# When the copies and the accumulations of summed weights are issued in a decoder layer, and how many splits stand ahead of the last pass's early sums

## The chip, the cores and the metric

The kernel runs on one core of a Trainium2 chip. Its time is in microseconds (us) of device time. TensorE does the matrix products, ScalarE and VectorE (ACT and DVE in the profile) the elementwise work, GpSimd (POOL) some of it and the DMAs that add while they write. SyncE (SP) issues nearly all other DMAs. All DMAs of the core run on the same 16 DMA engines.

## What is computed

One layer of a decoder, 256 tokens wide 2048, all in float32:

```python
h = rmsnorm(x, pre_mix_g);  proj = h @ w_in          # 2048 -> 4368 columns
o_a = sliding-window attention, o_b = forgetting attention, each rms-normalised
x = x + rmsnorm(concat(o_a, o_b) @ w_out, post_mix_g)
h = rmsnorm(x, pre_ffn_g)
u = causal_dwconv(h @ w_up, conv_w, conv_b)          # 2048 -> 2 * 5632
gate, val = split(u)
y = (gelu(gate) * val) @ w_down                      # 5632 -> 2048
out = x + rmsnorm(y, post_ffn_g)
```

## The kernel before

**Split weights.** TensorE works on pairs of reduced floats: each weight tile is loaded raw (float32, `w_load`, L88), ScalarE casts it to a high part (L143 in `w_split`, L343 in `split`), VectorE subtracts to get the low part (L146, L344), and a product is high by high, high by low and low by high. Five raw buffers and five pairs of split buffers turn in rings, so loads run ahead of TensorE until a ring is full. TensorE's order is the program's (`manual_schedule`, L48); the other engines are ordered by the framework's scheduler, apart from stretches that fix the order by hand: ScalarE, VectorE and GpSimd from L826 up to the first gate, and ScalarE, VectorE and SyncE from the last w_up group through the two column passes (L1199).

**The stages.** w_in: a start stage of four steps, then `proj_T` (L274) and plain loops (L662) for the three kinds of projection, with the attention of earlier heads woven in by `tick` and `later`. w_out: `out_half` (L735) twice; its last columns are done in a hand-ordered stretch (L826 to L873) in which `evac_b` (L763) scales and squares, GpSimd multiplies by the gain (L769), `mix_rstd` (L780) makes the reciprocal root (L214 on GpSimd), `residual` (L785) adds x (L787 on VectorE) and `turn` (L789) transposes on TensorE (L794). Then, twice, for one half of the 5632 rows each: eleven groups of w_up (`proj_T4`, L303: 32 high products at L315 and 32 low ones at L321 with four loads of 512 KB), each with a convolution (ScalarE L935, VectorE L937, GpSimd L938, ScalarE L942, VectorE L948 and L950), and after them two passes over w_down, one for each half of its columns (`column_pass`, L1017). While x goes into its next use, `x_dram` is written from ScalarE's queue (L991).

**Pair sums.** In a column pass rows come in pairs of 128-row blocks, eleven pairs to a half. For the six pairs in `FAST` seven block products are done in place of eight (`seven`, L1057), which needs sums of weight blocks. These are made in DRAM by DMA: `make_sums` (L70) returns eight steps for one pair. With b11, b12 (first block, left and right columns) and b21, b22 (second block), four copies on SyncE (L80) put b11, b22, b22 and b21 into t1, t3, t2 and t4, and four accumulating DMAs on GpSimd (L83) add b12 to t1, b12 to t3, t1 to t2 and t2 to t4. A full step moves 512 KB; in the first half t2 and t4 take only the first column pass, 256 KB.

**When a step is begun.** `w_load` counts its loads. From the 13th on, five loads of thirteen are followed by one step of the list `sum_steps`, copies and accumulations mixed in the order in which they depend on each other:

```python
        loads[0] += 1
        if loads[0] > SKIP and loads[0] * 5 % 13 < 5 and sum_steps and not paused[0]:
            tc.keep_in_program_order(sum_steps.pop(0)())
```

`paused` is set in the column passes, so no step is begun there, though their loads are counted. Loads 1 to 73 belong to w_in, 74 to 105 to w_out, 106 to 109 to the first gate; a half of w_up has 80 or more.

**The last pass.** Each pair is made ready by `prepare` (L1033): load, cast, subtract. In the second half's second pass the pairs go in the order 0, 2, 4, 1, 5, 6, 7, 3, 8, 9, 10, and the last three (`HOLD`) are kept: their products are done at the end, one output block after the other (`block`, L1094), so that blocks finish one by one. After the last fast pair (7), `ahead` makes the next two pairs ready, then `early_sums` (L1150) folds four banks into the output: a copy on ScalarE (L1161) and eight additions on VectorE (L1162 to L1169). The remaining pairs are made ready when the loop reaches them. Then VectorE adds bank 3 (L1240) and `down` (L1226) adds a block (L1229) and squares it on ScalarE (L1230); GpSimd multiplies by the last gain (`gain`, L1250, at L1253), `rstd_y` (L1264) makes `ry` (L1268), and `finish` (L1271) writes out.

Of the kernel before, what the change touches and what calls it, by code (L numbers as in the profile page):

```python
# [12 lines left out]
ALU = mybir.AluOpType  # L13
# [11 lines left out]
NEG = -1e30  # L25
FHALF = 22
HOLD = 3
SKIP = 12
FAST = (0, 2, 4, 5, 6, 7)


# [1 line left out]
def hybrid_layer(ctx: ExitStack, tc: tile.TileContext, x, pre_mix_g, w_in, b_forget, sinks,  # L33
# [3 lines left out]
    pe, act, dve, pool, sp = nc.tensor, nc.scalar, nc.vector, nc.gpsimd, nc.sync  # L37
# [12 lines left out]
    def bank(tag="acc"):  # L50
        return ps.tile([P, 512], F32, tag=tag, bufs=4, name="bank_" + tag)
# [13 lines left out]
    UNIT = 1024  # L65
    WB = 5

    pair_sums, sum_steps, loads, paused = {}, [], [0], [False]

    def make_sums(half, u):  # L70
        k = half * FHALF + 2 * u
        chunks = slice(0, 2) if half else slice(0, 1)
        t13, t24 = (tc.dram_tile([P, D], F32, name=n) for n in ("t13", "t24"))
        pair_sums[half, u] = t13, t24
        (t1, t3), (t2, t4), (b11, b12), (b21, b22) = (
            [w.rearrange("p (s x c) -> p s x c", s=2, x=2)[:, :, x, :] for x in range(2)]
            for w in (t13, t24, *(w_down[(k + a) * P:(k + a + 1) * P, :] for a in range(2))))

        def put(to, src, ch=slice(0, 2)):
            return lambda: sp.dma_start(to[:, ch, :], src[:, ch, :])  # L80

        def add(to, src, ch=slice(0, 2)):
            return lambda: pool.dma_start(to[:, ch, :], src[:, ch, :], accum_op=ALU.add)  # L83

        return [put(t1, b11), put(t3, b22), add(t1, b12), add(t3, b12), put(t2, b22, chunks),
                put(t4, b21, chunks), add(t2, t1, chunks), add(t4, t2, chunks)]

    def w_load(src, a, c, pin=False):  # L88
        raw = wp.tile([P, UNIT], F32, tag="raw", bufs=5, name="raw")
        i = sp.dma_start(raw[:, :a * c].rearrange("p (a c) -> p a c", a=a), src)  # L90
        if pin:
            tc.keep_in_program_order(i)
        loads[0] += 1
        if loads[0] > SKIP and loads[0] * 5 % 13 < 5 and sum_steps and not paused[0]:
            tc.keep_in_program_order(sum_steps.pop(0)())
        return raw, a, c

    last = []
    for half in range(2):
        for u in FAST:  # L100
            steps = make_sums(half, u)
            sum_steps += steps[:2] + last + steps[2:7]
            last = steps[7:]
    sum_steps += last

    LOW = 56

# [43 lines left out]
    def w_unit(src, a, c, keep=None):  # L151
        return w_split(w_load(src, a, c), keep=keep)
# [193 lines left out]
    with tc.tile_pool(name="mixp", bufs=1) as mp:  # L346
# [407 lines left out]
        hold = tc.tile_pool(name="hold", bufs=1)  # L754
# [61 lines left out]
        def out_cols(n, t, cs):  # L816
            b = bank()
            for k, hi, lo in kept[n]:
# [7 lines left out]
        order = tc.manual_schedule(engines={mybir.EngineType.Activation, mybir.EngineType.DVE,  # L826
                                            mybir.EngineType.Pool})
# [50 lines left out]
    with tc.tile_pool(name="ffn", bufs=1) as fp:  # L878
# [132 lines left out]
        def product(b, lh, ll, rhs, cols, first, last, to=None):  # L1011
            hi, lo = rhs
            for i, (a, r) in enumerate(((lh, hi), (lh, lo), (ll, hi))):
                pe.matmul(b[:, to] if to else b, a, r[:, cols], start=(first and i == 0),  # L1014
                          stop=(last and i == 2))

        def column_pass(G, sums, weights, some, order, k00, c0, load, parts, hold=1):  # L1017
# [7 lines left out]
            def of(k, t):  # L1025
                return G[k][:, t * P:(t + 1) * P], G[k][:, 256 + t * P:256 + (t + 1) * P]

            def first(bk):
                new = id(bk) not in started
                started.add(id(bk))  # L1030
                return new

            def prepare(u):  # L1033
                k = k00 + 2 * u
                if u not in some:
                    return [parts(load(w_rows(w_down, k + a, 1, c0, UNIT)), UNIT)
                            for a in range(2)]
                b11 = parts(load(w_rows(w_down, k, 1, c0, 512)), 512)
                w13, w24 = (w[:, c0:c0 + UNIT].rearrange("p (a c) -> p a c", a=1)
                            for w in weights[u])  # L1040
                r13 = load(w13)
                r2 = load(w_rows(w_down, k + 1, 1, c0, UNIT))
                f13 = parts(r13, UNIT)
                if ready_sums:
                    r24 = load(w24)
                else:
                    r24 = r13
                    dve.tensor_tensor(r24[:, left], r2[:, right], r13[:, left], op=ALU.add)
                    dve.tensor_tensor(r24[:, right], r2[:, left], r24[:, left], op=ALU.add)
                b2 = parts(r2, UNIT)  # L1050
                return b11, f13, b2, parts(r24, UNIT)

            def ahead(*us):
                for u in us:
                    ready[u] = prepare(u)
# [18 lines left out]
            def run(add_early):  # L1074
                early, late = ([bank(tag) for _ in range(4)] for tag in ("acc", "att"))
                banks.extend(zip(late, (0, 0, 1, 1), (left, right, left, right)))
                for i, u in enumerate(order):
                    forms = ready.pop(u) if u in ready else prepare(u)
                    if u in some:
                        seven(u, forms, *early, *late[:3])  # L1080
                        if u == fast[-1]:
                            ahead(*order[i + 1:i + 3])
                            add_early(*early)
                    elif i >= len(order) - hold:
                        held.extend((2 * u + a, forms[a]) for a in range(2))
                    else:
                        for a in range(2):
                            for bk, t, cols in banks:
                                product(bk, *of(2 * u + a, t), forms[a], cols, first(bk),
                                        hold > 1 and bk is late[3] and a == 1 and  # L1090
                                        u == plain[-1])
                return late
# [54 lines left out]
        def y_of(t, n):  # L1147
            return y_sb[:, t, n * 512:(n + 1) * 512]
# [24 lines left out]
        for half in range(2):  # L1173
# [5 lines left out]
            for g in range(FHALF // 2):  # L1179
# [36 lines left out]
                if g in FAST:  # L1216
                    i = FAST.index(g)
# [15 lines left out]
            for n, (_, run, block) in zip((0, 2), passes):  # L1233
# [8 lines left out]
                for i in range(4):  # L1242
# [4 lines left out]
                    else:  # L1247
                        dve.tensor_tensor(y_of(t, n + c), late[i], y_of(t, n + c), op=ALU.add)

        def gain(t, n, h=None, into=None):  # L1250
            cs = slice(0, 512) if h is None else slice(h * 256, h * 256 + 256)
            ys = y_sb[:, t, n * 512:(n + 1) * 512][:, cs]
            pool.tensor_tensor(ys if into is None else into, ys,  # L1253
                               gbf[n][:, cs], op=ALU.mult)
# [50 lines left out]
        last = fp.tile([P, 256], F32, tag="last", name="last")  # L1305
# [42 lines left out]
```

## Time and profile before

| what | us |
|---|---|
| median of 3 runs | 1058.95 (1058.43 to 1059.29) |
| the profiled execution | 1059.58 |
| its span, first to last instruction | 1057.9 |
| TensorE busy | 1043.1 |
| VectorE busy | 836.6 |
| ScalarE busy | 651.9 |
| GpSimd busy | 265.7 |

DMA engines moved 266.87 MB, 252 GB/s on average. TensorE's granted clock was 0.997 of full speed over the span.

The profile is one execution. A row of the timeline has start, duration, engine, line, operation, what is written from what, how many of them were merged, and in brackets how long the engine had been idle before and what ended that. A row of the waits has who waited for whom, the us in total, how often, and the longest. The chain of waits is followed back from the last instruction: at each step to what released it, or to the instruction before it on its engine. Queue q1 carries SyncE's DMAs, q0 those of GpSimd (the accumulations), q10 ScalarE's.

### The profile page before, as it was taken

To read this page: it belongs to the slowest core of one execution; us is meant where nothing else is said; L and a number is where in the kernel's file an instruction comes from. 1 tells how busy PE (TensorE), PEld (TensorE's weight loads), DVE (VectorE), ACT (ScalarE), POOL (GpSimd) and SP (SyncE) were. 2 spreads that over 40 slices of the span, in tenths; PEclk is the share of its full clock that TensorE was granted. 3 is DMA by queue.
4 is the path that set the end of the run, shared out by engine and by line. 5 is a ranking of instruction groups with operands and counts; after the bars stand their busy time and mean duration, and the time that the engine had idled before them with its cause. 6 is when DMAs were issued, how large, how long until landed. Compare 5 with 4: busy or idle time off the path is not lost.

```text
span 1057.9 us, 16559 instructions
## 1 busy us (share of the span) xinstructions
PE 1043.1 (99%) x5866; PEld 907.9 (86%) x5866; DVE 836.6 (79%) x1353; ACT 651.9 (62%) x1116; POOL 265.7 (25%) x304
## 2 busy tenths in 40 slices
PE   9999999999999999999999999999999999999995
PEld 7899988888888988888888888888888888888884
DVE  5989887887377797788796799857878788779885
ACT  6767667676466665665565666546555565558661
POOL 3254435442114132232231000013232231210005
PEclk9999999999999999999999999999999999999998
DMA  8768987977887999898989786879899897669792
GB/s 289 249 161 238 232 251 216 228 223 202 272 288 178 300 246 291 237 291 231 263 262 275 274 344 228 269 223 261 264 252 299 240 250 214 198 203 409 253 399 87
DMA packets 183806, 266.87 MB, mean 252 GB/s; under 512 B 9100, under 2 KB 133292, under 8 KB 182828
## 3 DMA queue, kind: packets, MB, share of 16 engines
q1 hardware_dynamic: 171200, 241.12, 69.0%
q0 software_dynamic: 11520, 22.02, 13.3%
q10 hardware_dynamic: 1004, 2.68, 0.7%
q8 instruction: 46, 0.75, 0.3%
q14 instruction: 36, 0.29, 0.1%
HBM read 261.45 MB, written 48.25 MB: 293 GB/s over the span
## 4 chain that ended last, share of the span: by engine, by line
PE 84%; DMA 5%; DVE 5%; issue 2%; ACT 2%; POOL 1%; SPq 0%; DVEq 0%; POOLq 0%; ACTq 0%
PE bank_acc L315 16%; PE bank_att L315 14%; PE bank_att L1014 11%; PE bank_acc L321 8%; PE bank_att L321 7%; PE bank_acc L284 7%; PE bank_acc L340 7%; PE bank_acc L1014 5%; PE bank_acc L289 4%; DMA raw<-in_w_out_dram 3%; PE bank_att L506 1%; DVE wlo L146 1%; PE bank_att L541 1%; DMA raw<-t 1%; PE bank_acc L977 1%
## 5 line engine op out<-in xcount | busy, mean ns | idle before, releaser
L146 DVE TENSOR_TENSOR wlo<-raw,whi 128x1024 fp32r<-128x1024 f32 (+3 forms) x271 | 336.6, 1254 | 109.0 <-ACT whi L143 101.1
L143 ACT CAST whi<-raw 128x1024 fp32r<-128x1024 f32 (+3 forms) x270 | 273.7, 1029 | 122.0 <-issue 42.7
L938 POOL TENSOR_TENSOR room<-room,rowf 128x256 f32<-128x256 f32 x88 | 96.5, 1116 | 357.6 <-DVE room L937 356.2
L315 PE MATMUL bank_acc<-hT,whi 128*128 128x512 f32 x736 | 173.3, 390 | 0.0
L315 PEld LDWEIGHTS bank_acc<-hT,whi 128*128 128x128 f32 x736 | 136.4, 188 | 27.4
L315 PE MATMUL bank_att<-hT,whi 128*128 128x512 f32 x640 | 150.6, 390 | 0.0
L315 PEld LDWEIGHTS bank_att<-hT,whi 128*128 128x128 f32 x640 | 118.7, 188 | 23.9
L1014 PE MATMUL bank_att<-whi,G 128*128 128x512 f32 x298 | 98.1, 389 | 0.0
L942 ACT ACTIVATE room<-room,cw 128x256 f32<-128x256 f32 x88 | 52.6, 601 | 67.5 <-POOL room L938 67.4
L321 PEld LDWEIGHTS bank_acc<-hT,wlo 128*128 128x128 f32 x736 | 89.3, 188 | 2.0
L321 PE MATMUL bank_acc<-hT,wlo 128*128 128x256 f32 x736 | 89.9, 279 | 0.0
L284 PE MATMUL bank_acc<-hT,whi 128*128 128x512 f32 x352 | 88.0, 395 | 0.0
L340 PE MATMUL bank_acc<-whi,oT 128*128 128x512 f32 (+1 forms) x272 | 81.8, 379 | 0.0
L321 PEld LDWEIGHTS bank_att<-hT,wlo 128*128 128x128 f32 x640 | 77.6, 188 | 1.7
L321 PE MATMUL bank_att<-hT,wlo 128*128 128x256 f32 x640 | 77.9, 279 | 0.0
L948 DVE SCALAR_TENSOR_TENSOR room<-room,cw 128x256 f32<-128x256 f32 x88 | 60.2, 687 | 18.3 <-ACT room L942 18.3
L344 DVE TENSOR_TENSOR wlo<-raw,whi 128x1024 fp32r<-128x1024 f32 (+1 forms) x61 | 66.7, 1117 | 8.8 <-ACT whi L343 7.8
L284 PEld LDWEIGHTS bank_acc<-hT,whi 128*128 128x128 f32 x352 | 63.3, 188 | 11.5
L343 ACT CAST whi<-raw 128x1024 fp32r<-128x1024 f32 (+1 forms) x61 | 57.5, 966 | 19.0 <-DMA raw<-in_w_down_dram 7.0
L1014 PEld LDWEIGHTS bank_att<-whi,G 128*128 128x128 f32 x298 | 55.9, 188 | 11.6
L340 PEld LDWEIGHTS bank_acc<-whi,oT 128*128 128x128 f32 x272 | 50.2, 188 | 9.4
L1014 PE MATMUL bank_att<-wlo,G 128*128 128x512 f32 x149 | 58.0, 389 | 0.0
(269 smaller groups left out, 1722.6 us busy)
## 6 DMA issues: line engine op xcount, KB each, us to landing
raw<-in_w_up_dram SPq DMA_DIRECT2D x176, 512.0 KB, 5.3
raw<-in_w_in_dram SPq DMA_DIRECT2D x51, 512.0 KB, 5.5
raw<-in_w_down_dram SPq DMA_DIRECT2D x49, 512.0 KB, 6.3
t<-in_w_down_dram SPq DMA_DIRECT2D x36, 512.0 KB, 6.9
raw<-in_w_out_dram SPq DMA_DIRECT2D x32, 512.0 KB, 6.9
t<-in_w_down_dram POOLq DMA_DIRECT2D x24, 512.0 KB, 10.8
raw<-t SPq DMA_DIRECT2D x18, 512.0 KB, 4.7
spare<-t SPq DMA_DIRECT2D x13, 512.0 KB
```

The lines of the kernel that those rows point to most:

```text
L143: i1 = act.copy(hi[:, cs], raw[:, cs])
L146: i2 = dve.tensor_tensor(lo[:, cs], raw[:, cs], hi[:, cs].bitcast(F32), op=ALU.subtract)
L284: pe.matmul(b, parts[u][0][:, a, m * P:(m + 1) * P], hT[:, kt, :], start=(kt == 0), stop=(kt == KT - 1))
L315: pe.matmul(b, parts[u][0][:, a, m * P:(m + 1) * P], hT[:, kt, :], start=(kt == 0), stop=(kt == KT - 1))
L321: pe.matmul(b[:, 256:512], parts[u][1][:, a, m * P:(m + 1) * P], hT[:, kt, 0:256], start=False, stop=False)
L340: pe.matmul(b, a, r[:, cols], start=(first and i == 0), stop=(last and i == 2))
L343: act.copy(hi, src)
L344: dve.tensor_tensor(lo, src, hi.bitcast(F32), op=ALU.subtract)
L938: pool.tensor_tensor(u[:, 2:258], u[:, 2:258], rowf, op=ALU.mult)
L942: act.activation(y, u[:, 2:258], AF.Identity, bias=cw[:, 3, ch:ch + 1], scale=cw[:, 2, ch:ch + 1])
L948: dve.scalar_tensor_tensor(y, u[:, 1:257], cw[:, 1, ch:ch + 1], y, op0=ALU.mult, op1=ALU.add)
L1014: pe.matmul(b[:, to] if to else b, a, r[:, cols], start=(first and i == 0), stop=(last and i == 2))
```

## The change

Copies and accumulations get a list each. A list is served only while the count of loads lies in a span, and each load there pays in a pace (9/8 or 9/16), counted in 256 KB; a step is begun when what is owed reaches its size (2, or 1 for the half steps). The copies' span is loads 13 to 90, the accumulations' loads 112 to 281, and these need the copies to be all begun. Loads of the column passes are no longer counted. Within the accumulations the last one of a pair (t2 to t4) stands behind the first one of the next pair.

In the pass with `hold` above 1, the second half's second, `ahead` now makes the next four pairs (3, 8, 9 and 10) ready ahead of the early sums, in place of two.

```diff
-SKIP = 12
+COPIES = (13, 91, 9 / 8)
+ADDS = (112, 282, 9 / 16)
...
         def put(to, src, ch=slice(0, 2)):
-            return lambda: sp.dma_start(to[:, ch, :], src[:, ch, :])
+            return ch.stop, lambda: sp.dma_start(to[:, ch, :], src[:, ch, :])
...
-        return [put(t1, b11), put(t3, b22), add(t1, b12), add(t3, b12), put(t2, b22, chunks),
-                put(t4, b21, chunks), add(t2, t1, chunks), add(t4, t2, chunks)]
+        copies.extend([put(t1, b11), put(t3, b22), put(t2, b22, chunks), put(t4, b21, chunks)])
+        return [add(t1, b12), add(t3, b12), add(t2, t1, chunks), add(t4, t2, chunks)]
+
+    def begin_some(steps, span):
+        begin, end, pace = span
+        if begin <= loads[0] < end:
+            owed[span] = owed.get(span, 0) + pace
+            while steps and owed[span] >= steps[0][0]:
+                size, step = steps.pop(0)
+                owed[span] -= size
+                tc.keep_in_program_order(step())
...
-        loads[0] += 1
-        if loads[0] > SKIP and loads[0] * 5 % 13 < 5 and sum_steps and not paused[0]:
-            tc.keep_in_program_order(sum_steps.pop(0)())
+        loads[0] += not paused[0]
+        if not paused[0]:
+            begin_some(copies, COPIES)
+            if not copies:
+                begin_some(adds, ADDS)
...
-            sum_steps += steps[:2] + last + steps[2:7]
-            last = steps[7:]
-    sum_steps += last
+            adds += steps[:1] + last + steps[1:3]
+            last = steps[3:]
+    adds += last
...
                         if u == fast[-1]:
-                            ahead(*order[i + 1:i + 3])
+                            ahead(*order[i + 1:i + (5 if hold > 1 else 3)])
                             add_early(*early)
```

More of the change, by code (lines that the diff above doesn't have):

```diff
@@ L66, in hybrid_layer @@
     WB = 5
-    pair_sums, sum_steps, loads, paused = {}, [], [0], [False]
+    pair_sums, loads, paused = {}, [0], [False]
+    copies, adds, owed = [], [], {}
     def make_sums(half, u):
@@ L79, in put @@
         def put(to, src, ch=slice(0, 2)):
-            return lambda: sp.dma_start(to[:, ch, :], src[:, ch, :])
+            return ch.stop, lambda: sp.dma_start(to[:, ch, :], src[:, ch, :])
         def add(to, src, ch=slice(0, 2)):
-            return lambda: pool.dma_start(to[:, ch, :], src[:, ch, :], accum_op=ALU.add)
-        return [put(t1, b11), put(t3, b22), add(t1, b12), add(t3, b12), put(t2, b22, chunks),
-                put(t4, b21, chunks), add(t2, t1, chunks), add(t4, t2, chunks)]
+            return ch.stop, lambda: pool.dma_start(to[:, ch, :], src[:, ch, :],
+                                                   accum_op=ALU.add)
+        copies.extend([put(t1, b11), put(t3, b22), put(t2, b22, chunks), put(t4, b21, chunks)])
[8 more added lines that the diff above has]
+                tc.keep_in_program_order(step())
     def w_load(src, a, c, pin=False):
@@ L1248, in hybrid_layer @@
                         dve.tensor_tensor(y_of(t, n + c), late[i], y_of(t, n + c), op=ALU.add)
+        assert not copies and not adds
         def gain(t, n, h=None, into=None):
```

## The prediction

> **What bounds the kernel now.** I read the page's first part, then TensorE's own waits, then the chain of waits around each of them, then the single engines in order of time.
>
> ```profile
> span 1057.9 us, 16559 instructions
> ## 1 busy us (share of the span) xinstructions
> PE 1043.1 (99%) x5866; PEld 907.9 (86%) x5866; DVE 836.6 (79%) x1353; ACT 651.9 (62%) x1116; POOL 265.7 (25%) x304
> ```
>
> A busy 99% proves little by itself, since the ends of matmuls are modelled. This is the whole list of what TensorE waited for (us in total, times, longest):
>
> ```profile
> PE bank_acc L200 <- DVE junk L195: 1.3, 1, 1.3
> PE bank_att L1014 <- DVE more L344: 1.2, 1, 1.2
> PE bank_acc L365 <- DMA x_in<-in_x_dram: 0.9, 1, 0.9
> PE bank_att L794 <- DVE x_sb L787: 0.6, 1, 0.6
> PE bank_att L553 <- DVE pl L344: 0.5, 1, 0.5
> PE bank_att L365 <- DMA x_in<-in_x_dram: 0.4, 1, 0.4
> ```
>
> Six waits, 4.9 us. Three (L200, L365 twice, 2.6 us) belong to the start, before any weight sum begins. L794 comes just before w_up, L1014 in the last pass; L553 is a busy stretch of VectorE in the projections. The change removes no matmul, so it can win only what lies in L794, L553 and L1014, and can lose wherever it makes TensorE wait anew. No w_up or w_down product waited, though DMA has much to do there. The profiled execution took 1059.58 us, 1.68 us over its span; the median of the runs is 1058.95. I work out differences on the profiled one and subtract them from the median.
>
> **Part 1: what leaves the stretch before w_up.** Until now every load up to the end of w_up could be followed by a copy or an accumulation. Afterwards the copies go with loads 13 to 90 and the accumulations with loads from 112. Loads 1 to 73 are w_in, 74 to 105 w_out, 106 to 109 the first gate units. So GpSimd issues no DMA in the projections and w_out at all. It did, on the chain that ends in the wait at L794:
>
> ```profile
> 319.04 2.61 POOL t L83 x3
> 321.65 2.57 POOL mix_sb L769 x2
> 324.22 0.53 POOL rmix L214
> 324.75 0.02 issue
> 324.77 0.76 DVE x_sb L787
> ...
> 329.77 0.87 PE bank_att L794 x8
> ```
> ```profile
> 324.56 0.39 PE L340 MATMUL bank_acc<-whi,oT 128*128 128x512 f32 x1
> 325.58 0.99 PE L794 MATMUL bank_att<-ident,x_sb 128*128 128x128 f32 x5 [0.63 <-DVE x_sb L787]
> ```
> ```profile
> 320.94 0.63 ACT L768 ACTIVATE junk<-mix_sb 128x512 bf16<-128x512 f32 x1 [2.02 <-DVE mix_sb L767]
> 321.48 0.19 ACT L768 ACTIVATION_READ_ACCUMULATOR junk<-mix_sb 128x1 f32 x1
> ```
>
> The chain's columns are start, duration, what. Three accumulations hold GpSimd for 2.61 us; two multiplications (L769), the rstd and the residual stand behind them. Without them the first L769 starts at 319.04. The second needs ScalarE's square, read out at 321.67, so it runs 321.7 to 323.0 at 1.28 each; rmix ends at 323.5, the residual at 324.3. Matmuls of 512 columns start 0.23 apart (see the last pass), so TensorE could turn to L794 at 324.79. It would find its input: 0.79 us come back. What is late next has 0.5 us of cover. The eight transposes there end 1.32 us after the first (two pieces of 0.66 in the chain) where the next eight need 0.87: the second residual is late as well, up to 0.45 more. I take **1.0 us**; bounds 0 (if ScalarE's square is late too) and 1.24. The wait at L553 I leave at 0 gained, 0.5 at most: it ends a run of splits and softmax work on VectorE, none of which the change takes away.
>
> **Part 2: DMA time.** A unit is 256 KB. There are 84 units of copies and 84 of accumulations. The price of a unit comes from the queues of 345 to 561 us (packets, MB, share of 16 engines):
>
> ```profile
> q1 hardware_dynamic: 45205, 48.44, 71.0%
> q0 software_dynamic: 3458, 6.63, 19.0%
> ```
>
> 216 us x 0.71 / 48.44 MB x 0.262 = 0.83 us for a unit loaded or copied, and 216 x 0.19 / 6.63 x 0.262 = 1.62 us for a unit accumulated. Four loads of 512 KB cost 6.64 us. Before, four loads took 1.54 steps with them, on average half copies, half accumulations of 1.75 units: 3.3 us, 9.9 in all. After, in the projections 4.5 units of copies: 3.7 us, 10.4 in all. In w_up 2.25 units accumulated: 3.65 us, 10.3 in all. TensorE's time for four w_up loads:
>
> ```profile
> 367.95 7.28 PE bank_att L315 x32
> 375.24 3.74 PE bank_att L321 x32
> ```
>
> 32 high and 32 low products, 11.02 us; a projection's four loads hold as many products and attention besides. So DMA stays below TensorE on both sides, at 93 to 94%, and five raw buffers with five split ones cover what comes in bunches. I cost this at nothing. SyncE issues the same copies only earlier, with no wait in front of its loads; in the projections GpSimd loses its queue of DMAs. In w_up an accumulation finds its copy long landed, but it holds GpSimd for 0.87 us (2.61 for three), once in 5 to 10 us where it was once in some 14: the convolution's multiplication (L938) queues behind it, ScalarE's L942 waits for that, and casts wait behind L942. The split buffers cover 0.87 us, here by at least the 1.2 us below; without that cover each would cost its 0.87. Between loads 91 and 111 nothing is begun. The place with the least cover is where w_up starts, while x_dram is written:
>
> ```profile
> 374.50 2.35 DVE L146 TENSOR_TENSOR wlo<-raw,whi 128x1024 fp32r<-128x1024 f32 x2
> ```
>
> The second split ends at 376.85, and its low products, the last 8 of the 32 from 375.24 on, start at 378.05: 1.2 us of cover.
>
> **Part 3: the last pass.** All eight splits of pairs 3, 8, 9 and 10 now come ahead of the eight early sums; before, four stood behind them. The order of buffers and loads is the same.
>
> ```profile
> 1032.70 1.09 PE L1014 MATMUL bank_att<-more,G 128*128 128x512 f32 x4
> 1034.95 0.74 PE L1014 MATMUL bank_att<-more,G 128*128 128x512 f32 x2 [1.15 <-DVE more L344]
> ```
> ```profile
> 1028.56 0.69 DVE L1169 TENSOR_TENSOR y_sb<-s,y_sb 128x512 f32<-128x512 f32 x1
> 1029.17 1.22 DVE L344 TENSOR_TENSOR wlo<-raw,whi 128x1024 fp32r<-128x1024 f32 x1
> ...
> 1032.58 2.31 DVE L344 TENSOR_TENSOR more<-spare,more 128x1024 fp32r<-128x1024 f32 x1
> 1034.82 0.68 DVE L1240 TENSOR_TENSOR y_sb<-bank_att,y_sb 128x512 f32<-128x512 f32 x1
> 1035.73 0.69 DVE L1229 TENSOR_TENSOR y_sb<-bank_att,y_sb 128x512 f32<-128x512 f32 x1 [0.23 <-PE bank_att L1014]
> ...
> 1039.85 0.69 DVE L1229 TENSOR_TENSOR y_sb<-bank_att,y_sb 128x512 f32<-128x512 f32 x1 [2.30 <-PE bank_att L1014]
> ```
> ```profile
> 1026.30 1.05 ACT L343 CAST more<-spare 128x1024 fp32r<-128x1024 f32 x1 [0.20 <-DMA spare<-in_w_down_dram]
> ```
> ```profile
> 1031.89 4.15 POOL L1253 TENSOR_TENSOR y_sb<-y_sb,gbc_ffn 128x512 f32<-128x512 f32 x2 [94.61 <-DMA gbc_ffn<-in_post_ffn_g_dram]
> 1037.25 2.54 POOL L1253 TENSOR_TENSOR y_sb<-y_sb,gbc_ffn 128x512 f32<-128x512 f32 x2 [1.21 <-ACT junk L1230]
> 1041.63 0.56 POOL L1268 TENSOR_TENSOR ry<-rv,mhalf 128x1 f32<-128x1 f32 x1 [1.85 <-DVE rv L1266]
> ```
>
> Four matmuls from 1032.70 at 0.23 reach 1033.61; the next began at 1034.95, so TensorE lost 1.34 us to the last split, which ended at 1034.89. After, that split follows its cast, which waits for its load: 1027.35, and 1.22 more is 1028.6, four us before TensorE wants it. The wait is gone. Next late is VectorE's own queue: early sums from 1028.6, eight at 0.69 to 0.73 to 1034.4, L1240 to 1035.1, then block 0's addition (L1229), about as before. Block 1's products end 1.34 earlier, at 1038.5; from its addition the chain runs over ry to the outputs, so the end moves with it. Two gains of GpSimd (1031.89) fall beside the sums: the split at 1032.58 took 2.31 instead of 1.22 beside them, 1.09 lost. If two sums pay that, L1229 of block 0 ends at 1038.0, GpSimd's pair behind it (0.73 and 2.54) at 1041.3, ry moves only from 1041.63 to 1041.3, and the gain shrinks to 0.3. Bounds 0.3 and 1.34; since one such delay costs the end nothing, I take **1.3 us**.
>
> The Trainium skill ("SBUF — State Buffer", section "Who interferes with whom") says that a VectorE instruction with two SBUF inputs and a GpSimd instruction that reads SBUF exclude each other, the later one blocking for the whole of the other. By that rule four of the eight sums can be hit, but only two gains are ready to hit them; the 2.31 agrees with it.
>
> Sum: 1.0 + 1.3 = 2.3 us; 1058.95 - 2.3 = **1056.7**. A measurement of this kernel can tell about 0.2%, 2.1 us, from no change, so the forecast lies just past that line.
>
> **Rivals.** *B, w_up starts with a wait.* By the old rule loads 114 to 120 began two copies of 512 KB and an accumulation of 256 KB (4.9 us of DMA); by the new one two accumulations of 512 and one of 256 KB (8.1). The extra 3.2 us meet 1.2 us of cover: up to 2.0 us of new wait near 370 us, 1056.7 to 1058.7. For it: x_dram's write crowds the same stretch. Against it: no copies stand ahead of the loads in their own queue any more. The Trainium skill ("DMA: Bandwidth & Descriptors", "Queues, rings and completion order") says that an engine takes turns between queues packet by packet; by that rule loads are slowed for as long as an accumulation runs, which speaks for B. No run here shows it separately.
>
> *C, the last pass gives back little*, because both gains hit the early sums: 0.3 in place of 1.3, 1057.7.
>
> *D, accumulations overfill w_up: slower.* It decides from (11.02 - 6.64) / 2.25 = 1.95 us a unit. In the window 46 to 110 us accumulations were dearer:
>
> ```profile
> q0 software_dynamic: 688, 1.31, 16.3%
> ```
>
> 64 x 0.163 / 1.31 x 0.262 = 2.09 us a unit. At that price four loads need 11.34 us, 0.32 too many; accumulations last 149 loads, 37 groups, 12 us; less some 6 us that the buffers lend, and less the 2.3 gained, about 1063 (1060 to 1067). Against it: 1.62 was measured in w_up itself.
>
> **How the numbers follow.** Forecast (both waits go) 0.46, B 0.24, C 0.14, D 0.14, anything else 0.02. Within the forecast the first gain's bounds decide which side of 2.1 us it falls: 0.36 of its 0.46 beyond, with 0.04 of B and C where L553 goes too: faster 0.40. D and a little else: slower 0.16. Same 0.44. Range: below, both gains at their upper bounds and L553 (1.24 + 1.34 + 0.5) give 1055.9; above, B's and C's ends and the start of D: 1060.0.
>
> **What would show it.** Right: TensorE's list of waits without L794 and the last L1014; no accumulation on GpSimd before about 340 us; the copies done by about 260; the step from w_up's first product to w_down's unchanged; VectorE's sums behind all splits. Wrong: a wait of TensorE at L315 or L321 on wlo or whi (B near 370, D again and again), DMA at a full share through w_up, or ry no earlier against the last product (C).

## The result, and the profile after

| | before | after |
|---|---|---|
| median | 1059.86 us (12 runs, 1058.43 to 1062.12) | 1057.27 us (12 runs, 1056.56 to 1059.2) |
| profiled execution | 1059.58 us, span 1057.9 | 1057.50 us, span 1055.8 |

The ratio is 0.9976, 95% interval 0.9967 to 0.9985: 2.5 us less (1.6 to 3.5). That is clear of no change; the interval reaches across the line of 2.1 us that the prediction drew. Lines of the code have moved: L83 is L85 after, and from `w_load` on 12 to 16 are to be added (L794 is L808, L1014 is L1028, L1253 is L1269).

TensorE's whole list of waits in the kernel after, us in total, times, longest:

```profile
PE bank_acc L214 <- DVE junk L209: 1.3, 1, 1.3
PE bank_att L567 <- DVE pl L358: 0.5, 1, 0.5
PE bank_acc L379 <- DMA x_in<-in_x_dram: 0.2, 1, 0.2
```

Both waits that the change could remove are gone, the turn's and the last pass's, and between 340 and 1000 us no new one has come. The rest stands in the start stage and at L567 (the former L553), and these were there before.

The chain around the turn, start, duration, what:

```profile
325.62 0.87 PE bank_att L808 x8
326.49 2.88 PE bank_acc L354 x24
329.37 0.87 PE bank_att L808 x8
...
337.74 1.75 PE bank_att L808 x16
```

Transposes go at 0.87 for eight everywhere; before, the first eight took 1.31 (0.66 twice) and the last sixteen 2.20. GpSimd and VectorE in front of it:

```profile
321.85 1.29 POOL L783 TENSOR_TENSOR mix_sb<-mix_sb,gbc_mix 128x512 f32<-128x512 f32 x1 [4.14 <-ACT junk L782]
323.10 0.55 POOL L228 TENSOR_TENSOR rmix<-rv,mhalf 128x1 f32<-128x1 f32 x1
```
```profile
320.21 0.75 DVE L781 SCALAR_TENSOR_TENSOR mix_sb<-bank_acc,rg,mix_sb 128x512 f32<-128x512 f32 x1 [1.42 <-PE bank_acc L354]
323.68 2.74 DVE L801 SCALAR_TENSOR_TENSOR x_sb<-mix_sb,rmix,x_sb 128x512 f32<-128x512 f32 x4 [1.53 <-POOL rmix L228]
```

No DMA stands on GpSimd; the last gain waits for ScalarE's square, that for VectorE's L781, and that for TensorE itself. What the first gains wait for in the kernel before comes with the run only_last. The copies on SyncE (48 of them, the first begun at 34.6 us, the last at 256.9) and the queues in w_up, 345 to 561 us (packets, MB, share of 16 engines):

```profile
L82 SPq DMA_DIRECT2D t<-in_w_down_dram x48: 496/506/1342, 34.6 to 256.9; - x48
```
```profile
q1 hardware_dynamic: 42306, 42.22, 60.1%
q0 software_dynamic: 5536, 10.49, 33.2%
```

A unit of 256 KB accumulated costs 216 x 0.332 / 10.49 x 0.262 = 1.79 us here, 1.62 before. The two queues together take 93.3% of the engines' time, as the prediction worked out for w_up.

The last pass on VectorE and GpSimd:

```profile
1027.87 1.23 DVE L358 TENSOR_TENSOR more<-spare,more 128x1024 fp32r<-128x1024 f32 x1
1029.01 0.68 DVE L1176 TENSOR_TENSOR y_sb<-s,y_sb 128x512 f32<-128x512 f32 x1
...
1034.02 1.44 DVE L1181 TENSOR_TENSOR y_sb<-s,y_sb 128x512 f32<-128x512 f32 x1
...
1036.22 0.94 DVE L1183 TENSOR_TENSOR y_sb<-s,y_sb 128x512 f32<-128x512 f32 x1
...
1037.80 0.68 DVE L1243 TENSOR_TENSOR y_sb<-bank_att,y_sb 128x512 f32<-128x512 f32 x1
```
```profile
1032.36 5.95 POOL L1269 TENSOR_TENSOR y_sb<-y_sb,gbc_ffn 128x512 f32<-128x512 f32 x4 [95.94 <-DMA gbc_ffn<-in_post_ffn_g_dram]
1039.57 0.56 POOL L1284 TENSOR_TENSOR ry<-rv,mhalf 128x1 f32<-128x1 f32 x1 [1.26 <-DVE rv L1282]
```

The last split takes 1.23 us at 1027.87, where it took 2.31 at 1032.58; two sums of two SBUF inputs are stretched beside the gains instead (1.44 and 0.94 against 0.68). ry comes 2.06 us earlier on the profile's clock, but 0.29 us later against the last product (6.00 us ahead of it in place of 6.29).

**Where the time went, in one table.** Each number is the profiled execution's time from one TensorE milestone to the next, less the same stretch of before, in us. The first column runs up to w_out's first product. Most of it arises in the first 12 us, where x's loads and the first matmuls differ from execution to execution by up to 1.3 us, in only_last too, which leaves that stage as it was; this is why spans of single executions must not be compared here. The second column runs to w_up's first product behind the last transposes of the turn (L794, now L808). In the stretches that have no column no execution differs by more than 0.01 us. The last column is the ratio of the fast runs to those of the kernel before beside them, with its interval.

| kernel | start to w_out | w_out to w_up | w_up, first half | last pass | behind it | ratio |
|---|---|---|---|---|---|---|
| after | +0.66 | -1.51 | 0 | -1.51 | +0.28 | 0.9976 (0.9967 to 0.9985) |
| only_last | +0.91 | -1.51 | 0 | -1.51 | -0.03 | 0.9982 (0.9974 to 0.9991) |
| only_dma | +0.59 | -1.51 | 0 | -0.16 | +0.01 | 0.9985 (0.9976 to 0.9993) |
| copies_to_111 | -0.07 | -1.50 | 0 | -1.52 | +0.01 | 0.9971 (0.9962 to 0.9981) |
| adds_from_91 | +0.68 | +3.01 | 0 | -1.51 | +0.01 | 1.0016 (1.0004 to 1.0029) |
| three_pairs | +1.14 | -1.50 | 0 | -0.35 | +0.01 | 1.0003 (0.9990 to 1.0016) |
| gains_first | +0.77 | -1.51 | 0 | -1.11 | +0.04 | 0.9976 (0.9964 to 0.9989) |
| two_pairs_late_gains | +0.33 | -1.50 | 0 | -1.08 | +1.50 | 0.9989 (0.9980 to 0.9998) |
| late_gains | -0.34 | -1.51 | +4.58 | -1.51 | +1.48 | 0.9991 (0.9979 to 1.0004) |
| adds_1_2 | +2.09 | -1.50 | 0 | -1.52 | +0.05 | 0.9978 (0.9969 to 0.9988) |
| adds_3_4 | +1.26 | -1.51 | 0 | -1.51 | +0.04 | 0.9967 (0.9950 to 0.9983) |
| adds_15_16 | -0.31 | -1.50 | +18.06 | -1.52 | +0.02 | 1.0142 (1.0126 to 1.0159) |
| adds_9_8 | +1.03 | -1.50 | +36.14 | -1.51 | +0.05 | 1.0261 (1.0221 to 1.0302) |

One piece of the first column lies behind the start stage. In six of the twelve executions with the new transfers (only_dma, copies_to_111, gains_first, two_pairs_late_gains, adds_1_2, adds_9_8) TensorE waits a second time at L567, near 59 us, and loses 0.33 to 1.03 us; in the change's own execution and in the two without the new transfers it doesn't. The largest, in adds_1_2, where the wait that all executions have is 0.5 us of the sum:

```profile
PE bank_att L567 <- DVE pl L358: 1.4, 2, 0.9
```

The copies now stand more densely beside that stage. Whether they make this wait isn't shown: two executions of the old transfers are too few, and no run moves the copies away from there.

### The profile page after: what moved, and what is told of

Same layout as the page of the kernel before. It is cut to its first block, busy times and chain, and to the rows that moved or that the text cites. A ratio compares the mean times of both kernels' runs of the same rounds, so it can differ in the third digit from the quotient of the medians.

```text
span 1055.8 us, 16539 instructions
## 1 busy us (share of the span) xinstructions
PE 1043.7 (99%) x5866; PEld 910.1 (86%) x5866; DVE 832.7 (79%) x1353; ACT 652.4 (62%) x1116; POOL 269.4 (26%) x304
## 4 chain that ended last, share of the span: by engine, by line
PE 90%; DMA 4%; DVE 2%; ACT 1%; POOL 1%; issue 1%; DVEq 0%; SPq 0%; POOLq 0%; ACTq 0%
PE bank_acc L329 16%; PE bank_att L329 14%; PE bank_acc L354 12%; PE bank_att L1028 11%; PE bank_acc L335 8%; PE bank_att L335 7%; PE bank_acc L298 7%; PE bank_acc L1028 5%; PE bank_acc L303 4%; DMA raw<-in_w_down_dram 1%; PE bank_att L520 1%; DMA gbc_ffn<-in_post_ffn_g_dram 1%; PE bank_att L555 1%; DMA raw<-t 1%; DVE wlo L160 1%
## 5 line engine op out<-in xcount | busy, mean ns | idle before, releaser
L160 DVE TENSOR_TENSOR wlo<-raw,whi 128x1024 fp32r<-128x1024 f32 (+3 forms) x271 | 332.2, 1238 | 99.8 <-ACT whi L157 93.0
L1028 PE MATMUL bank_att<-whi,G 128*128 128x512 f32 x298 | 98.1, 389 | 0.0
L1028 PEld LDWEIGHTS bank_att<-whi,G 128*128 128x128 f32 x298 | 55.9, 188 | 11.6
L1028 PE MATMUL bank_att<-wlo,G 128*128 128x512 f32 x149 | 58.0, 389 | 0.0
```

The lines of the kernel that those rows point to most:

```text
L160: i2 = dve.tensor_tensor(lo[:, cs], raw[:, cs], hi[:, cs].bitcast(F32), op=ALU.subtract)
```

## The experiments

The theory at the outset: three accumulations on GpSimd make the turn's wait, and splits behind the early sums make the last pass's. Rivals: the bytes of copies and accumulations beside w_out's loads make the first; the gain beside the split makes the second.

**only_last: the last pass's edit alone, on the kernel before.**

```diff
-                            ahead(*order[i + 1:i + 3])
+                            ahead(*order[i + 1:i + (5 if hold > 1 else 3)])
```

> The kernel before with the last pass's edit alone: while more than one pair is still held, four pairs are split ahead instead of two; the copies and accumulations are as before. Theory (each edit acts in its own stretch): TensorE's wait in w_down's last pass, 1.34 us before, goes, and the last product comes about 1.5 us earlier, as it did between the two kernels (2.36 us in all less the 0.85 us already won by w_up's first product). Some 0.2 to 0.3 us of it is given back behind the last product, because the sums of the second pairs now run beside GpSimd's gains. So about 1.2 us less than before, a ratio of 0.9989, and the wait at the turn (L794) stands as it did, 0.5 to 0.8 us. Rival (the gain needs the new transfers too): below 0.4 us less than before.

Measured: 1058.75 us against 1060.16, ratio 0.9982. The last pass gives its 1.51 us alone. But the wait at the turn is absent too, though GpSimd's order is that of before, row by row. The accumulations are there:

```profile
318.40 0.81 POOL L83 DMA_DIRECT2D t<-t  x1
318.95 2.07 POOL L83 DMA_DIRECT2D t<-in_w_down_dram  x2
320.09 3.50 POOL L769 TENSOR_TENSOR mix_sb<-mix_sb,gbc_mix 128x512 f32<-128x512 f32 x2
323.36 0.75 POOL L214 TENSOR_TENSOR rmix<-rv,mhalf 128x1 f32<-128x1 f32 x1
```

They begin at 318.40 where they began at 319.04 before, 0.64 earlier, while TensorE in this execution is 0.91 later. Two expectations missed here: the turn's wait did not stay, and the last pass gave nothing back behind the last product. The first matters: the turn's wait isn't a fixed 1.5 us of the old kernel, but depends on who is ahead in an execution. The cover, the time at which TensorE could turn to the transposes (0.23 us after the start of its last product) less the end of the first residual, says it in one number:

| execution | accumulations ahead of rmix | cover, us |
|---|---|---|
| before | three in a row | -0.73 |
| only_last | three in a row | +0.81 |
| adds_from_91 | five, spread | -2.67 |
| after and the ten other kernels with the new transfers | none | +1.01 or +1.02 each |

Why GpSimd is so late in the old kernel the rows of the kernel before show one step further back:

```profile
304.42 9.09 DVE L129 TENSOR_TENSOR wlo<-raw,whi 128x1024 fp32r<-128x1024 f32 x6
...
314.90 2.07 DVE L767 SCALAR_TENSOR_TENSOR mix_sb<-bank_acc,rg,mix_sb 128x512 f32<-128x512 f32 x3
```
```profile
316.54 2.55 POOL L769 TENSOR_TENSOR mix_sb<-mix_sb,gbc_mix 128x512 f32<-128x512 f32 x2 [7.52 <-ACT junk L768]
```

VectorE does seven splits of w_out's weights in a row (the seventh at 313.76, behind a load that landed at 312.60) before it scales the columns that the third and fourth gain need. So these gains start at 316.54, 8.0 us before TensorE's last product ahead of the turn, and the three accumulations come behind them. In only_last it is 315.91 and 9.6 us; after the change it is 310.48 and 14.7 us. Read from these rows, the wait of the old kernel had two conditions: gains that were late already, and 2.61 us of accumulations behind them. No run takes away the first alone.

**only_dma: the new transfers alone** (the same line undone in the kernel after).

> The changed kernel with the last pass's edit undone (two pairs are split ahead again); the copies are all in the projections and the accumulations all in w_up. Theory: w_up's first product comes 0.8 to 1.5 us earlier than before, the wait at the turn is gone, and the wait of 1.34 us in the last pass is back; the end is 0.8 to 1.5 us earlier than before, a ratio of 0.9986 to 0.9992. Rival (the transfers give nothing at the end and all of the gain is the last pass's): within 0.3 us of before.

Measured: 1058.51 against 1060.16, ratio 0.9985; w_up starts 1.51 us earlier counted from w_out, and the last pass keeps its wait:

```profile
PE bank_att L1028 <- DVE more L358: 1.0, 1, 1.0
```
```profile
1031.50 2.31 DVE L358 TENSOR_TENSOR more<-spare,more 128x1024 fp32r<-128x1024 f32 x1
```

As expected. By the ratios the last pass's edit alone gives 1.9 us (1.0 to 2.8) and the transfers alone 1.6 us (0.7 to 2.5), together 2.5 (1.6 to 3.5).

**adds_from_91 and copies_to_111: what makes the turn's wait.** One puts accumulations back ahead of rmix, the other puts copies back beside w_out's loads.

```diff
-ADDS = (112, 282, 9 / 16)
+ADDS = (91, 282, 9 / 16)
```
```diff
-COPIES = (13, 91, 9 / 8)
+COPIES = (13, 112, 7 / 8)
```

> The changed kernel, but its accumulations begin in w_out's second half, at a pace of 9/16 from load 91 on: five of them stand between the gains ahead of rmix on GpSimd, and all copies are done by then. Theory (GpSimd's time ahead of rmix makes the turn's wait): at about 0.87 us of GpSimd an accumulation, up to 4 us are put in front of rmix, against 2.61 us before; TensorE waits at the turn again, at least the 0.5 to 0.8 us of before and up to 2 us more, so 1 to 3 us slower than the changed kernel. Rival (the copies' and accumulations' bytes beside w_out's loads made the wait): the accumulations alone are less than half of what was moved there in all, so the wait is absent or below 0.3 us, and the time is within 0.5 us of the changed kernel's.

> The changed kernel, but its copies are spread to load 111 at a pace of 7/8, so that they go on through w_out beside its loads; no accumulation stands in front of rmix on GpSimd. Theory (GpSimd's time ahead of rmix makes the turn's wait): no wait at the turn; the time is that of the changed kernel, within 0.4 us. Rival (bytes beside w_out's loads make the wait): TensorE waits at the turn or at a load of w_out, 0.5 to 1.5 us, and the time is that much longer.

Measured: 1061.62 (1.0016) and 1057.05 (0.9971). With accumulations the turn waits 2.6 us; with copies, and DMA 98 to 104% busy from 284 to 314 us, it doesn't wait at all, cover 1.01. So the copies' bytes alone don't make the wait, and that rival falls. But neither run has the late gains of the old kernel: the third and fourth start at 309.57 in copies_to_111 and at 310.51 in adds_from_91. What made them late, copies and accumulations together beside w_out's loads or their order, no run separates. adds_from_91 makes its wait in another way:

```profile
316.86 1.19 POOL L85 DMA_DIRECT2D t<-in_w_down_dram  x1
323.49 0.81 POOL L85 DMA_DIRECT2D t<-t  x1 [5.44 <-DMA t<-t]
324.04 2.80 POOL L783 TENSOR_TENSOR mix_sb<-mix_sb,gbc_mix 128x512 f32<-128x512 f32 x2
326.52 0.84 POOL L228 TENSOR_TENSOR rmix<-rv,mhalf 128x1 f32<-128x1 f32 x1
```

Here it isn't GpSimd's 0.81 us of issuing that hurts, but its waiting: an addition of one sum to another is begun only once the sum that it reads has landed; GpSimd stood 5.44 us for it, and the gains stood behind. The stretch is 4.5 us longer than the change's, where 1 to 3 were expected: behind the wait of 2.6 us TensorE's granted clock was 0.50 from 330 to 332 us.

**three_pairs and gains_first: two other ways through the last pass.**

```diff
-                            ahead(*order[i + 1:i + (5 if hold > 1 else 3)])
+                            ahead(*order[i + 1:i + (4 if hold > 1 else 3)])
```

gains_first moves the four loads of gbc_ffn ahead of the loads of x_back (L1296 to L1301).

> The changed kernel, but three pairs, not four, are split ahead of the early sums in the last pass, so that the last pair's splits stand behind sums. Theory (TensorE waits for what stands behind the sums): the wait of the last pass is back in part, 0.7 to 1.4 us, and the end is 0.5 to 1.3 us later than the changed kernel's. Rival (two pairs were too few and three are enough): no wait, and the time within 0.3 us of the changed kernel's.

> The changed kernel, but the four loads of the last gains (gbc_ffn) stand ahead of the reloads of x in SP's order, so GpSimd's gains behind w_down's last products start about 3 to 5 us earlier and run beside VectorE's splits, no longer beside the early sums. Theory (the 0.28 us that is given back behind the last product comes from the sums of two SBUF inputs that took 1.44 and 0.94 us beside the gains, against 0.69 us): the sums take 0.69 us each, the last down addition follows its product at once, and the end is about 0.3 us earlier than the changed kernel's. Rival (the splits, with SBUF inputs too, are hit in place of the sums): they take 2.0 us or more in place of 1.23 us, TensorE waits in the last pass, and the end is 0 to 1.5 us later. A third: the reloads of x come later and hold up what uses them, which would show as a wait of VectorE or ScalarE for x at the end.

Measured: 1060.27 (1.0003) and 1057.79 (0.9976). With three pairs the last split is stretched as before and TensorE waits 0.8 us:

```profile
1031.87 2.31 DVE L358 TENSOR_TENSOR more<-spare,more 128x1024 fp32r<-128x1024 f32 x1
```

The profiled execution of three_pairs (1058.87) is its fastest, and its end, counted from w_out, comes 0.9 us later than the change's, within the 0.5 to 1.3 expected; by the ratios three_pairs is 2.9 us slower than the change, and what its other runs, up to 1063.33, lost, no trace shows. In gains_first the first two gains no longer come at 1031 but at 994 and 997, beside other splits:

```profile
997.65 1.71 POOL L1269 TENSOR_TENSOR y_sb<-y_sb,gbc_ffn 128x512 f32<-128x512 f32 x1 [1.12 <-DMA gbc_ffn<-in_post_ffn_g_dram]
```
```profile
998.13 3.44 DVE L358 TENSOR_TENSOR wlo<-spare,whi 128x1024 fp32r<-128x1024 f32 x2
```
```profile
1000.49 0.50 PE L1028 MATMUL bank_acc<-wlo,G 128*128 128x512 f32 x1
```

Two splits take 3.44 us in place of 2.45, and TensorE, whose matmuls start 0.23 apart, starts this one 0.26 late and the next 0.11: nearly all of the 0.40 us that the last pass lacks against the change. The gain behind the last product (+0.28 to +0.04) is as expected, but kernels that share the change's last pass (adds_3_4, adds_1_2, copies_to_111) have it too, at +0.01 to +0.05: the 0.28 is chance, two sums hit in the change's execution where one is in theirs. Both together leave the time where it was. The third possibility, a late x, didn't come.

**two_pairs_late_gains and late_gains: the split's place or the gain beside it?**

```diff
-        gain(0, 0)
-        gain(0, 1)
         block(0)
         down(0, 2, late[0])
         gain(0, 2)
-        gain(1, 0)
+        gain(0, 0)
+        gain(0, 1)
...
         gain(0, 3)
+        gain(1, 0)
         gain(1, 1)
```

> The kernel with the new transfers and two pairs split ahead, as in the run where the last pass's edit was undone, but GpSimd's first two gains, and the one of block (1, 0), stand behind the gain that waits for block 0's sum, so that no gain runs while VectorE still splits. Theory now (the wait in the last pass is the last split's own stretching by the gain beside it, 2.31 us in place of 1.22 us, and not the place of the sums): that split takes 1.22 us, TensorE's wait at L1028 falls from 1.0 us to 0 to 0.2 us, and the last product comes about 1.1 us earlier than in that run, 0.3 to 0.5 us later than the changed kernel's at the most. Rival (the prediction's: the splits are late because the sums stand ahead of them): the wait stays, 0.8 to 1.0 us.

> The changed kernel (four pairs split ahead) with GpSimd's first gains moved the same way. Theory (the 0.28 us given back behind the last product is the sums' stretching, 1.44 and 0.94 us in place of 0.69 us): at most one sum is still stretched, the addition of block 1 follows its product at once, no wait of TensorE is added, and the end comes 0.2 to 0.3 us earlier than the changed kernel's, counted from w_up's first product. Rival (the gains, now begun some 2.5 us later, hold up ry and the output): the end is 0.3 to 1.5 us later.

Measured: 1059.09 (0.9989) and 1058.55 (0.9991). With two pairs and no gain beside the splits, these stand behind the sums exactly as before, and the wait at L1028 is no longer in the list:

```profile
1031.47 1.22 DVE L358 TENSOR_TENSOR more<-spare,more 128x1024 fp32r<-128x1024 f32 x1
```
```profile
1035.04 3.78 POOL L1269 TENSOR_TENSOR y_sb<-y_sb,gbc_ffn 128x512 f32<-128x512 f32 x3 [98.94 <-ACT junk L1244]
```

The split is back at 1.22 us and the last product comes 1.08 us earlier than before, against 0.16 in only_dma. So with the place left as it was, taking the gain away wins 0.92 of the 1.35 us between only_dma and the change; the place alone, without a gain beside it, costs the other 0.43. The edit of the last pass wins all 1.35, because splits that stand ahead of the sums are over before the gains begin. The late gains themselves are no improvement: the end comes 1.5 us later behind the last product, in both kernels, since VectorE's outputs now fall beside a gain, and the last additions and the second ry stand behind them (the rival). late_gains shows one thing more, near 531 us in w_up, whose instructions are the change's own:

```profile
PE bank_acc L335 <- DVE wlo L160: 2.5, 2, 2.3
```
```profile
530.00:532.00 2.00, 0.90 (x8) 0.70 (x6) 1.03 (x4) 1.58 (x3) 0.00 (x0) 1.00 0.66 200
532.00:534.00 2.00, 0.81 (x6) 0.81 (x7) 2.00 (x4) 1.37 (x3) 0.45 (x1) 0.95 0.29 103
534.00:536.00 2.00, 2.00 (x8) 1.71 (x8) 2.00 (x2) 0.70 (x2) 2.00 (x3) 0.50 0.77 250
536.00:538.00 2.00, 2.00 (x8) 1.59 (x7) 1.61 (x5) 2.00 (x3) 1.54 (x2) 0.69 0.83 256
```

(Stretch, length, busy time of PE, PEld, DVE, ACT, POOL, then the granted clock, the DMA share and GB/s.) A split came too late, TensorE waited 2.5 us, and then ran at half its clock: 4.58 us in all. Other executions came near it: the smallest margin of a split in w_up's first half, from its end to the product that reads it, behind the second group, is 0.5 to 2.9 us in six of the other seven executions at this pace (2.9 in the change's, 1.4 in only_dma, 0.8 in copies_to_111, 0.5 in three_pairs) and 3.6 in adds_from_91; with the old transfers it is 1.0 (before) and 0.7 (only_last). Why the split fell behind in this execution alone isn't settled; the table's ratio of late_gains holds whatever of it other executions had.

**adds_3_4, adds_15_16, adds_9_8, adds_1_2: how many accumulations w_up bears.** Each changes the last number of ADDS alone.

> The changed kernel with its accumulations at a pace of 3/4 of a load instead of 9/16: three beside each group of four loads of w_up in place of 2.25. By the rule of overfilling that was weighed before: four loads are 6.64 us of all DMA engines and three accumulations at 1.62 us are 4.86 us, together 11.5 us in a group of 11.02 us; 0.48 us too much in each of some 28 groups is 13 us, of which the buffers cover about 6 us, so about 7 us slower than the changed kernel, with waits on loads of w_up. At the 1.79 us an accumulation that the changed kernel's w_up shows it is 12.0 us a group and about 20 us. Rival (the accumulations queue behind each other without holding the loads up): within 0.5 us of the changed kernel.

> The changed kernel with its accumulations at a pace of 9/8, double: 4.5 beside each group of four loads of w_up until all are done. By the rule of overfilling: 6.64 + 4.5 x 1.62 = 13.9 us of transfers in a group of 11.02 us, 2.9 us too much in each of some 19 groups, 54 us less about 6 us of buffers, so some 45 us slower than the changed kernel, with waits on w_up's loads. Rival (the accumulations queue behind one another on their own queue and take only the share that the loads leave): no more than 2 us slower.

> The changed kernel with accumulations at a pace of 15/16, 3.75 units beside each group of four loads, between the two paces tried. By the rule of overfilling, at the 1.52 us a unit that the pace of 9/8 showed: 6.6 + 3.75 x 1.52 = 12.3 us of transfers in a group of 11.02 us, 1.3 us too much in each of 72 / 3.75 = 19 groups, 25 us less about 6 us that the buffers cover, so 15 to 20 us slower than the changed kernel, with TensorE waiting for w_up's splits and its clock granted at about a half behind each wait of over 3 us. Rival (the loss at 9/8 comes from the waits' length, and shorter shortages are absorbed): below 6 us.

> The changed kernel with accumulations at a pace of 1/2 in place of 9/16: two units of 256 KB beside each group of four loads of w_up. In the changed kernel's profiled run the smallest margin of a split in w_up's first half is 2.8 us at the second group and then 2.9 to 3.7 us at every second group from 437 to 525 us; in one profiled run with the same instructions in w_up it was gone at 524 us, and 4.6 us were lost there. Theory (the accumulations bring the splits that near to late): 6.4 + 2 x 1.76 = 9.9 us of transfers in a group of 11.02 us instead of 10.4 us, the margins behind the second group are 4 us or more, TensorE has no wait in w_up, and the median is the changed kernel's or up to 0.5 us less (a ratio to the kernel before of 0.997 to 0.998). Rival (the last sums of the first half are now accumulated too late for w_down, some 25 us later than before, at 571 us): a wait for a load of them at L1028 between 580 and 690 us, 1 us or more slower.

Measured: 1057.86 (0.9967) at 3/4, 1087.79 (1.0261) at 9/8, 1075.42 (1.0142) at 15/16 and 1057.12 (0.9978) at 1/2. The queue of accumulations from 348 to 500 us at paces 3/4, 15/16 and 9/8, and TensorE's waits at 9/8:

```profile
q0 software_dynamic: 5151, 9.76, 41.8%
```
```profile
q0 software_dynamic: 5973, 11.35, 46.3%
```
```profile
q0 software_dynamic: 6352, 12.06, 46.9%
```
```profile
PE bank_acc L335 <- DVE wlo L160: 12.6, 5, 4.2
PE bank_att L335 <- DVE wlo L160: 8.6, 5, 4.1
```

That is 1.71, 1.63 and 1.55 us a unit (152 us x share / MB x 0.262). At these three paces, the more is issued, the less of the engines' time a unit takes. 3 units beside four loads cost nothing, where 7 us or more were expected; 3.75 cost 18.1 us in the profiled execution (17.6 against the change by the ratios), where 15 to 20 were expected; and 4.5 cost 36.1 in the profiled execution, the slowest of its four (30 by the ratios), where some 45 were expected. It wasn't the buffers that bore the 3 units: the engines were 1.04 busy from 348 to 500 us, and still the margins of each group's last split stood at 4.8 to 5.7 us from 411 to 532 us; the smallest, later, is 2.2. So a unit's share of the engines is no fixed price, and the sum of the prices (8 units loaded at 0.78 and 3 at 1.71, 11.4 us against 11.02) puts the limit somewhat too low. The rivals (accumulations that only queue) hold at 3/4 and fall for the two high paces. At 9/8 the waits are 21 us of the 36. Much of the rest is clock:

```profile
456.00:460.00 4.00, 3.07 (x11) 2.87 (x12) 3.63 (x5) 2.12 (x4) 2.71 (x3) 0.54 0.78 237
460.00:464.00 4.00, 4.00 (x12) 3.10 (x11) 3.67 (x6) 3.74 (x6) 2.23 (x3) 0.61 0.80 204
464.00:468.00 4.00, 4.00 (x19) 3.27 (x18) 2.90 (x4) 1.61 (x3) 0.00 (x0) 1.00 1.04 171
```

Behind waits of 1.6 and 3.0 us at 451 to 457, 12 matmuls fit in 4 us, then 19 again. At 1/2 the smallest margin behind the second group is 4.5 us in the first half, no load of a sum was waited for, and the ratio is that of the change within its interval. By its margins it should be safer against a stretch like the one of late_gains, but its 10 runs go to 1058.69 and the change's 12 to 1059.2, too little to show that.

## Why the prediction was right, and where it was not

**The forecast (both waits go, 2.3 us) held**: 2.5 us (1.6 to 3.5) by the ratio, 2.74 by the profiled executions from w_out on (1.51 + 1.51 - 0.28). The time of 1056.7 was taken off a median of three runs that lay 0.9 us below the later median of twelve.

**Part 1, 1.0 us with bounds 0 to 1.24: the place was right, the size too small.** The table's 1.51 is 0.6 at the turn's first transpose, 0.45 in the first eight, and 0.45 in the last sixteen at 338 us. The first two, 1.07 together, the prediction had at 1.0 (0.79 from start to start, and "up to 0.45 more" from end to end, so that its bound of 1.24 counts some of it twice); the third, the same late residuals one turn further on, it didn't look for. That accumulations ahead of rmix are needed for the wait stood the test: without them the chain to the turn hangs on TensorE alone and the cover is 1.01 us in eleven executions out of eleven; with them it was -0.73, +0.81 and -2.67. That 2.61 us of issuing are enough did not: only_last has the three accumulations and no wait, and adds_from_91 has its wait from an accumulation that stood 5.44 us. The prediction took the wait as a property of the kernel and did not ask why the gains ahead of the accumulations were late. The old kernel pays in some executions, and how many isn't known from two profiles; that the gain of the medians came out near one read from such an execution is partly luck.

**Part 2, nothing: right for w_up in the change's execution, with little to spare, and open for the projections.** late_gains lost 4.58 us in w_up with the same instructions there, and six executions have the second wait at L567, 0.33 to 1.03 us, that the prediction had at nothing; what makes either isn't shown. Rival B (a new wait near 370 us) didn't come. The prediction let the accumulations begin with load 114; on GpSimd they stood behind other work, the first began at 363.8 us, and the margin of the split near 371 is 4.6 us where it had 1.2 of cover (1.0 by the product's own row, which starts at 377.88). Rival D (accumulations overfill w_up) is wrong at this pace and right as a mechanism: the prediction set its point at 1.95 us a unit for 2.25 units, 4.4 us of accumulations a group, and the runs put it between 3 units of 1.71 (5.1 us, borne) and 3.75 of 1.63 (6.1 us, 18 us lost), so at a little more than the difference to TensorE's 11.02 us. The 6 us that it took for what the buffers lend stands on no row; in the changed kernel's w_up the margins reach 11.8 us for a group's first split and 5.7 for its last. The dear 2.09 us that spoke for D is met nowhere in w_up.

**Part 3, 1.3 us: right in size, with half of its reason.** 1.51 at the last product, 1.23 at the end in the change's execution, 1.5 in the others with its last pass and its gains. The step that fell short is the one from "TensorE lost 1.34 us to the last split" to the splits' place behind the sums: with the place kept, the split's own 2.31 us beside a gain made 0.92 us of it, and the place 0.43. The prediction quoted that row but used it only for rival C. The edit won the whole because it moves the split away from both. C itself came in a mild form: two sums were hit for 0.75 and 0.26 us, and 0.28 reached the end, in this profiled execution and in no other with the same order. The sign set for C (ry no earlier against the last product) could not have told it from the forecast, by which ry moves with that product. The Trainium skill ("SBUF — State Buffer", "Who interferes with whom") states the exclusion that was drawn on; the split's 2.31 us in three executions with a gain beside it, and 1.22 in those without, agree with it.

## What to carry to other kernels

Before crediting a wait to the order of a queue, look at the length of the instruction that ended it: here a split of 1.22 us that took 2.31 beside another engine made two thirds of the wait, and curing the stretching alone won back those two thirds. Take a wait found in one profile as one draw: compare the cover (how long before its use an input is ready) over several executions, for an edit can be worth the whole wait in one and nothing in the next. Do the same for the stretches that an edit loads anew, even where one profile shows no wait. Here transfers added beside a stage cost nothing up to a sum of engine time a little above the stage's own (11.4 us in 11.02), and much at the next step tried (12.5), the more since long waits also cost clock.

## What the runs showed of the hardware

A long wait of TensorE cost more than itself: after 2.3 us of waiting (late_gains) the granted clock was 0.50 for some 2 us and 0.69 for 2 more, after 2.6 us (adds_from_91) 0.50 and 0.84, and at pace 9/8 21 us of waits came with 36 us of loss. After the waits of 0.6 and 1.2 us in the kernel before, and of 1.6 us at pace 9/8, it stayed at 1.00. The Trainium skill ("TensorE: Matmul & The Clock Gate", "Part 1: The HAM clock gate") says that the clock falls to half after an idle window of about 3.4 us; here a wait of 2.3 us, in a stretch of 4 us with 1.7 us of matmuls, was enough.

An accumulating DMA takes 1.55 to 1.79 us of all engines for 256 KB in w_up, twice what a load takes, and falling from 1.76 to 1.55 as 2.25 to 4.5 of them go with four loads (348 to 500 us). On GpSimd one takes 0.8 to 1.5 us to issue, mostly 0.9, and one that must wait for another holds up all that is queued behind it, 5.44 us here.
